# One of sixteen convolution taps per pass of the ConvFFN loop: from VectorE to ScalarE and GpSimd

## The chip, the cores and the metric

The kernel runs on one core of a Trainium2 chip. The metric is the device time of one execution in microseconds (us), as the median of several runs. The engines are TensorE (PE in the rows, its weight loads PEld), VectorE (DVE), ScalarE (ACT), GpSimd (POOL) and SyncE (SP), whose queue issues the DMAs spoken of here.

## What is computed

The kernel is one layer of a diffusion backbone: a token mixer (Fourier and gated recurrence), then a convolutional feed-forward block, then a final norm. The change lies in the feed-forward block:

```python
D_MODEL, SEQ, GRID_W, D_FF = 1024, 1024, 64, 2816     # 1024 tokens are a grid of 16 x 64

def dwconv2d(u, w, bias):          # 3x3, one filter per channel, zero padding
    ...
    return y + bias

def conv_ffn(h, rows, w_up, conv_w, conv_b, w_down):
    b, n, _ = h.shape
    u = (h @ w_up).reshape(b, rows, n // rows, 2 * D_FF)
    u = dwconv2d(u, conv_w, conv_b).reshape(b, n, 2 * D_FF)
    gate, val = jnp.split(u, 2, axis=-1)
    return (jax.nn.gelu(gate) * val) @ w_down
```

## The kernel before

The 2 x 2816 channels are handled in 22 pairs (`NP = 22`) of a gate tile and a value tile, each 128 channels by 1024 tokens. `ffn()` runs one **pass** n for each pair. A pass overlaps three stages of neighbouring pairs:

- **The product of pair n** (`up_product`, L1526). The up-projection of a gate and a value block is done by a Strassen-like scheme of seven products, i = 0 to 6, each of 12 matmuls (float32 split in a high and a low part). They go into two PSUM tiles, `ug` and `uv`, of which two pairs exist, so that pair n and pair n - 1 are held at once. Product 6 of a pair is made late, as the second product of the next pass. The order on TensorE in pass n is therefore (n,0), (n-1,6), (n,1), (n,2), (n,3), (n,4), (n,5). ScalarE copies some results (rows `ug<-ug`, `uv<-ug`, `p<-uv`, `u<-uv` of L131), and VectorE finishes each tile with one addition, the **join** (`up_join`, L1542): `ug<-ug,p` after product 4, `uv<-uv,u` after product 5. Product (n-1,6) waits for the join of `uv`.
- **The convolution of pairs n and n - 1** (`up_conv`, `conv`). ScalarE writes the centre tap and the bias into an accumulator in SBUF (L1552, for `uv` after product (n-1,6), for `ug` after the join). The other eight taps are `scalar_tensor_tensor` instructions on VectorE (L1564), which read PSUM and add into the accumulator. In pass n, VectorE runs: eight taps of the gate tile n - 1, five of the value tile n - 1, join of `ug`, three of the value tile n - 1, join of `uv`. Pass n is counted here from the join of `uv` of pair n - 1 to that of pair n.
- **The product of gate and value of pair n - 2** (`glu`, L1574): one GpSimd multiplication and a store of 512 KB to DRAM, `G<-s`, issued by SyncE.

Beside these, every pass prepares the weights of pair n + 1 (`up_split`): for each of the seven products ScalarE rounds 512 columns to float32r (`s<-s` of L131) and GpSimd subtracts to get the low part (L138). It also forms sums of weights of pair n + 2 on GpSimd (L1474, L1476, L1478, L1492) and loads two weight blocks (L1465).

**The slots.** Every tile in SBUF that these stages use (weights, their high and low parts, accumulators) takes one of 48 equal slots of 4 KB per partition (33 and 15, `Slots`). A freed slot goes to the end of a queue, and `get` takes the slot that has been free for longest. The order is fixed when the program is written, not at run time: an instruction that first writes a slot waits until all readers of its former tile are done, a store by DMA among them. In `glu` the value accumulator (`va`) and then the gate accumulator (`ga`) are given back; the last reader of `ga` is the store.

The order on each engine is the order in which this code issues its instructions; no scheduler moves them.

Of the kernel before, what the change touches and what calls it, by code (L numbers as in the profile page):

```python
# [10 lines left out]
AF = mybir.ActivationFunctionType  # L11
OP = mybir.AluOpType

S, D, C = 1024, 1024, 256
# [3 lines left out]
NP = FF // 128  # L18
# [94 lines left out]
class K:  # L113
# [1429 lines left out]

    def up_conv(self, n, x):
        u = self.U[n]
        u[x + "a"], u[x + "t"] = self.conv(u[x], n if x == "g" else NP + n)

    def conv(self, ps, ti):

        nc = self.nc  # L1550
        acc = self.sl.get([128, S], any_=True)
        nc.scalar.activation(acc, ps, AF.Identity, bias=self.par["fcb"][:, ti:ti + 1], scale=self.fcw(4, ti))  # L1552
        a3 = acc.rearrange("p (y x) -> p y x", y=GH)
        p3 = ps.rearrange("p (y x) -> p y x", y=GH)
        taps = deque()
        for dy in (-1, 0, 1):
            for dx in (-1, 0, 1):
                if dy == 0 and dx == 0:
                    continue
                y0, y1, x0, x1 = max(0, -dy), GH - max(0, dy), max(0, -dx), GW - max(0, dx)  # L1560
                o = a3[:, y0:y1, x0:x1]
                i = p3[:, y0 + dy:y1 + dy, x0 + dx:x1 + dx]
                taps.append(lambda o=o, i=i, w=self.fcw((dy + 1) * 3 + dx + 1, ti):
                            nc.vector.scalar_tensor_tensor(o, i, w, o, op0=OP.mult, op1=OP.add))  # L1564
        return acc, taps

    def gelu(self, n):
        g = self.U[n]["ga"]
# [2 lines left out]
    def glu(self, n):  # L1571

        nc, u = self.nc, self.U[n]
        nc.gpsimd.tensor_tensor(u["ga"], u["ga"], u["va"], op=OP.mult)  # L1574
        self.sl.free(u["va"])
        nc.sync.dma_start(self.G[n], u["ga"])
        self.sl.free(u["ga"])
        del self.U[n]
# [416 lines left out]
```

## Time and profile before

| | us |
|---|---|
| median of 3 runs | 1557.04 (1555.39 to 1558.95) |
| the profiled execution | 1557.34 |
| its span | 1555.5 |
| VectorE busy | 1215.6 (78%) |
| TensorE busy | 1408.2 (91%), granted clock 0.966 of full speed on average |
| GpSimd busy | 755.1 (49%) |
| ScalarE busy | 669.3 (43%) |

The feed-forward loop with its 22 pairs lies between about 835 us and 1275 us of the span. The shares over the whole span mix it with stages of other kinds, so the loop has to be read by itself, one pass at a time.

### The profile page before, as it was taken

To read this page: it belongs to the slowest core of one execution; us is meant where nothing else is said; L and a number is where in the kernel's file an instruction comes from. 1 tells how busy PE (TensorE), PEld (TensorE's weight loads), DVE (VectorE), ACT (ScalarE), POOL (GpSimd) and SP (SyncE) were. 2 spreads that over 40 slices of the span, in tenths; PEclk is the share of its full clock that TensorE was granted. 3 is DMA by queue.
4 is the path that set the end of the run, shared out by engine and by line. 5 is a ranking of instruction groups with operands and counts; after the bars stand their busy time and mean duration, and the time that the engine had idled before them with its cause. 6 is when DMAs were issued, how large, how long until landed. Compare 5 with 4: busy or idle time off the path is not lost.

```text
span 1555.5 us, 17031 instructions
## 1 busy us (share of the span) xinstructions
PE 1408.2 (91%) x6333; PEld 1126.9 (72%) x6333; DVE 1215.6 (78%) x1265; ACT 669.3 (43%) x968; POOL 755.1 (49%) x504
## 2 busy tenths in 40 slices
PE   5999999998999689979967999999999988989983
PEld 4788888877887678868845777777777767768862
DVE  5768677855116986495687999999999989799795
ACT  6566777663110213342255444444444434445441
POOL 2211311122002452392088777788777726886760
PEclk9999999999999899989988999999999998999996
DMA  9211111101115444413321112222211166422622
GB/s 374 94 34 34 35 34 41 41 28 55 41 54 180 136 126 160 154 41 122 111 80 54 66 61 78 82 82 82 82 63 64 51 243 230 183 75 102 230 88 103
DMA packets 52787, 155.21 MB, mean 100 GB/s; under 512 B 5781, under 2 KB 10192, under 8 KB 52704
## 3 DMA queue, kind: packets, MB, share of 16 engines
q1 hardware_dynamic: 51264, 151.76, 27.4%
q10 hardware_dynamic: 1184, 2.11, 0.4%
q8 instruction: 50, 0.82, 0.2%
q0 software_dynamic: 256, 0.25, 0.1%
q14 instruction: 33, 0.27, 0.1%
HBM read 131.29 MB, written 22.81 MB: 99 GB/s over the span
## 4 chain that ended last, share of the span: by engine, by line
DVE 36%; PE 13%; issue 6%; ACT 2%; POOL 1%; DMA 1%; SPq 0%; DVEq 0%; ACTq 0%; POOLq 0%
DVE s L1564 23%; PE big L194 6%; PE dn L1792 6%; DVE s L138 2%; POOL s L138 1%; DVE ug L1542 1%; DVE s L1713 1%; DVE uv L1542 1%; DVE s L1710 1%; DVE s L1225 1%; PE uv L1526 1%; DVE s L1784 1%; DMA s<-G 1%; ACT s L131 1%; DVE s L1726 1%
## 5 line engine op out<-in xcount | busy, mean ns | idle before, releaser
L138 POOL TENSOR_TENSOR s<-s,s 128x512 fp32r<-128x512 f32 (+1 forms) x288 | 462.0, 1621 | 332.4 <-ACT s L131 259.9
L194 PE MATMUL big<-s,s 128*128 128x512 f32 (+2 forms) x2352 | 559.2, 396 | 10.3 <-DVE s L138 6.5
L194 PEld LDWEIGHTS big<-s,s 128*128 128x128 f32 (+2 forms) x2352 | 438.0, 189 | 115.7 <-DVE s L138 7.8
L131 ACT ACTIVATE s<-s 128x512 fp32r<-128x512 f32 (+2 forms) x406 | 263.0, 697 | 259.8 <-DVE mid L912 61.9
L1526 PE MATMUL ug<-s,s 128*128 128x512 f32 x1056 | 263.9, 398 | 24.3 <-ACT uv L131 13.4
L138 DVE TENSOR_TENSOR s<-s,s 128x512 fp32r<-128x512 f32 (+2 forms) x150 | 189.8, 1274 | 92.1 <-ACT s L131 64.7
L1526 PEld LDWEIGHTS ug<-s,s 128*128 128x128 f32 x1056 | 197.7, 189 | 79.1 <-ACT uv L131 22.0
L1792 PE MATMUL dn<-s,s 128*128 128x512 f32 x924 | 227.9, 408 | 29.9 <-DVE s L138 15.5
L1792 PEld LDWEIGHTS dn<-s,s 128*128 128x128 f32 x924 | 180.0, 196 | 77.7 <-DVE s L138 17.5
L1564 DVE SCALAR_TENSOR_TENSOR s<-ug,rest,s 128x945 f32<-128x945 f32 (+2 forms) x176 | 214.9, 1221 | 5.3
L1564 DVE SCALAR_TENSOR_TENSOR s<-uv,rest,s 128x945 f32<-128x945 f32 (+2 forms) x176 | 214.8, 1220 | 4.6
L1526 PE MATMUL uv<-s,s 128*128 128x512 f32 x792 | 199.9, 402 | 15.3 <-DVE uv L1542 14.0
L1526 PEld LDWEIGHTS uv<-s,s 128*128 128x128 f32 x792 | 149.5, 191 | 59.1 <-DVE uv L1542 23.4
L782 POOL TENSOR_TENSOR s<-s,s 128x1280 f32<-128x1280 f32 x8 | 25.2, 3152 | 190.9 <-ACT s L778 190.9
L899 POOL TENSOR_TENSOR s<-s,s 128x1024 f32<-128x1024 f32 x8 | 21.1, 2641 | 127.4 <-PE big L194 120.7
L1474 POOL TENSOR_TENSOR s<-s,s 128x512 f32<-128x512 f32 x22 | 28.6, 1301 | 63.6 <-DMA s<-in_ffn_w_up_b_dram 63.6
L131 ACT ACTIVATE p<-uv 128x512 f32<-128x512 f32 x22 | 13.2, 599 | 105.5 <-PE uv L1526 105.5
L885 DVE TENSOR_TENSOR s<-big,s 128x1024 f32<-128x1024 f32 x8 | 9.8, 1224 | 61.1 <-PE big L194 61.1
L745 DVE SCALAR_TENSOR_TENSOR s<-big,par,s 128x1023 f32<-128x1023 f32 (+1 forms) x24 | 30.8, 1282 | 34.2 <-ACT s L742 33.6
L1574 POOL TENSOR_TENSOR s<-s,s 128x1024 f32<-128x1024 f32 x22 | 53.4, 2427 | 5.5 <-DVE s L1564 5.5
L1552 ACT ACTIVATE s<-uv,rest 128x1024 f32<-128x1024 f32 x22 | 26.6, 1208 | 48.2 <-POOL s L138 33.6
L777 ACT ACTIVATE s<-big,rest 128x1024 f32<-128x1024 f32 x32 | 35.7, 1117 | 24.6 <-PE big L194 17.8
(231 smaller groups left out, 1537.8 us busy)
## 6 DMA issues: line engine op xcount, KB each, us to landing
s<-in_mod_w_dram SPq DMA_DIRECT2D x48, 512.0 KB, 4.7
s<-in_ffn_w_up_b_dram SPq DMA_DIRECT2D x44, 512.0 KB, 4.3
s<-in_w_in_b_dram SPq DMA_DIRECT2D x32, 512.0 KB, 4.3
s<-G SPq DMA_DIRECT2D x55, 256.0 KB, 3.2
G<-s SPq DMA_DIRECT2D x22, 512.0 KB, 2.6
s<-in_ffn_w_down_dram SPq DMA_DIRECT2D x22, 512.0 KB, 5.8
s<-in_x_dram SPq DMA_DIRECT2D x16, 512.0 KB, 5.4
s<-G SPq DMA_DIRECT2D x11, 512.0 KB, 5.7
```

What stands on the lines that cost most here:

```text
L131: self.nc.scalar.activation(out, in_, AF.Copy)
L138: (self.nc.vector if eng == "dve" else self.nc.gpsimd).tensor_tensor(out, a, b, op=OP.subtract)
L194: return [lambda x=x: nc.tensor.matmul(x[0], x[1], x[2], start=x[3], stop=x[4]) for x in calls]
L745: nc.vector.scalar_tensor_tensor(u[:, lo:hi], z[:, lo + s:hi + s], tap[t], u[:, lo:hi], op0=OP.mult, op1=OP.add)
L777: nc.scalar.activation(lat, ps, AF.Sigmoid, bias=col)
L1474: p.tensor_tensor(u["x"][:, L], rg[:, L], rv[:, L], op=OP.subtract)
L1526: nc.tensor.matmul(o, x, y, start=first, stop=k == 3 and m == 2, skip_group_check=not fresh)
L1542: self.nc.vector.tensor_tensor(o, o, p, op=OP.add)
L1552: nc.scalar.activation(acc, ps, AF.Identity, bias=self.par["fcb"][:, ti:ti + 1], scale=self.fcw(4, ti))
L1564: nc.vector.scalar_tensor_tensor(o, i, w, o, op0=OP.mult, op1=OP.add))
L1574: nc.gpsimd.tensor_tensor(u["ga"], u["ga"], u["va"], op=OP.mult)
L1792: nc.tensor.matmul(bank[j], x, z, start=first and m == 0, stop=end and m == 2, skip_group_check=not check)
```

## The change

For the value tiles of pairs 0 to 20, the first of the eight taps (dy = -1, dx = -1: 15 rows of 63 elements, 945 per partition) is no longer a VectorE instruction. ScalarE multiplies the shifted PSUM tile by the tap's weight and writes the result into a slot of its own (`t`, L1567 of the new numbering, right behind the centre tap). GpSimd adds `t` to the accumulator at the beginning of `glu` (L1583), then multiplies as before (L1585), and `t` is given back ahead of `va` and `ga`. Pair 21 keeps all taps on VectorE.

```diff
     def up_conv(self, n, x):
         u = self.U[n]
-        u[x + "a"], u[x + "t"] = self.conv(u[x], n if x == "g" else NP + n)
-
-    def conv(self, ps, ti):
+        u[x + "a"], u[x + "t"], u[x + "r"] = self.conv(u[x], n if x == "g" else NP + n, x == "v" and n < NP - 1)
+
+    def conv(self, ps, ti, shared=False):
...
-        taps = deque()
+        taps, rest = deque(), None
...
+                if shared and rest is None:
+                    t = self.sl.get([128, S], any_=True)
+                    m = t[:, 0:(y1 - y0) * (x1 - x0)].rearrange("p (y x) -> p y x", y=y1 - y0)
+                    nc.scalar.activation(m, i, AF.Copy, scale=self.fcw((dy + 1) * 3 + dx + 1, ti))
+                    rest = o, m, t
+                    continue
...
-        return acc, taps
+        return acc, taps, rest
...
     def glu(self, n):
 
         nc, u = self.nc, self.U[n]
+        if u["vr"] is not None:
+            o, m, t = u["vr"]
+            nc.gpsimd.tensor_tensor(o, o, m, op=OP.add)
+            self.sl.free(t)
         nc.gpsimd.tensor_tensor(u["ga"], u["ga"], u["va"], op=OP.mult)
         self.sl.free(u["va"])
         nc.sync.dma_start(self.G[n], u["ga"])
```

The slots that the tiles get are other ones too, and with them the waits. On ScalarE, in the middle of the loop, one pass from the copy that follows product (n,1) stands as below before the change. `s1176`, `s1178`, `s1182`, `s1186` are the high parts of the weights for products 1 to 4 of the next pair; L1569 is the gelu, L1552 the centre tap of the gate tile, `u3` the copy that the join of `uv` needs. Names of semaphores in brackets say which engine or DMA queue an instruction waits for.

```order
L1552 ACTIVATE s1174_6810<-uv_6619,rest_93 128x1024 [waits DVE_49,PE_49,Pool_49]
L131 ACTIVATE uv_6766<-ug_6765 128x512 [waits PE_49]
L131 ACTIVATE s1176_6825<-s1160_6716 128x512 [waits Pool_49]
L131 ACTIVATE s1178_6840<-s1144_6620 128x512
L131 ACTIVATE p5_6858<-uv_6766 128x512 [waits PE_49,Activation_49]
L131 ACTIVATE s1182_6860<-s1145_6622 128x512
L131 ACTIVATE s1186_6882<-s1144_6620 128x512 [waits Pool_49]
L1569 ACTIVATE s1164_6741<-s1164_6741 128x1024 [waits DVE_49]
L1552 ACTIVATE s1188_6888<-ug_6765,rest_93 128x1024 [waits DMAHW4_49,DVE_49]
L131 ACTIVATE u3_6905<-uv_6766 128x512 [waits PE_49]
```

Here the wait for a DMA (`DMAHW4`, the store of `ga` of this pass's `glu`) stands at the centre tap `s1188`, whose slot was that `ga`. After the change the same place reads as follows; L1553 is the centre tap, L1567 the new tap, L1576 the gelu, and `s1188`, `s1190`, `s1195`, `s1199` are the high parts for products 1 to 4.

```order
L1553 ACTIVATE s1185_6821<-uv_6628,rest_93 128x1024 [waits DVE_49,PE_49]
L1567 ACTIVATE s1186_6823<-uv_6628,rest_93 128x945
L131 ACTIVATE uv_6777<-ug_6776 128x512 [waits PE_49]
L131 ACTIVATE s1188_6838<-s1171_6728 128x512 [waits Pool_49]
L131 ACTIVATE s1190_6853<-s1153_6629 128x512 [waits PE_49]
L131 ACTIVATE p5_6872<-uv_6777 128x512 [waits PE_49,Activation_49]
L131 ACTIVATE s1195_6874<-s1154_6631 128x512 [waits Pool_49]
L131 ACTIVATE s1199_6896<-s1153_6629 128x512 [waits DMAHW4_49,Pool_49]
L1576 ACTIVATE s1175_6753<-s1175_6753 128x1024 [waits DVE_49]
L1553 ACTIVATE s1201_6902<-ug_6776,rest_93 128x1024 [waits DVE_49]
L131 ACTIVATE u3_6918<-uv_6777 128x512 [waits PE_49]
```

Three waits are new: `s1190` waits for TensorE (its slot held the weights that product (n,2) of this very pass reads), `s1195` for GpSimd (its slot was `t`), and `s1199` for the store of `ga` of this pass's `glu`, whose slot it takes. The wait for the store has moved from the centre tap to an instruction ahead of the gelu.

On GpSimd, from the low part for product 2 on, the same stretch of a pass stands like this before the change (`L1574` is the multiplication of `glu`):

```order
L138 TENSOR_TENSOR s1178_6840<-s1144_6620,s1178_6840 128x512 [waits PE_49,Activation_49]
L1492 TENSOR_TENSOR s1144_6620<-s1144_6620,s1160_6716 128x512 [waits Pool_49]
L1574 TENSOR_TENSOR s1140_6594<-s1140_6594,s1150_6663 128x1024 [waits DMAHW6_49,DVE_49]
L138 TENSOR_TENSOR s1182_6860<-s1145_6622,s1182_6860 128x512 [waits PE_49,Activation_49]
L1474 TENSOR_TENSOR s1184_6863<-s1168_6767,s1169_6769 128x512 [waits DMAHW3_49,DMAHW2_49,PE_49]
L138 TENSOR_TENSOR s1186_6882<-s1144_6620,s1186_6882 128x512 [waits Activation_49]
```

and like this after it, with the new addition (L1583) ahead of the multiplication (L1585):

```order
L138 TENSOR_TENSOR s1216_7002<-s1179_6778,s1216_7002 128x512 [waits Activation_49]
L1492 TENSOR_TENSOR s1179_6778<-s1179_6778,s1197_6877 128x512 [waits Pool_49]
L1583 TENSOR_TENSOR s1185_6821<-s1185_6821,s1186_6823 128x15x63 [waits DVE_49]
L1585 TENSOR_TENSOR s1175_6753<-s1175_6753,s1185_6821 128x1024 [waits Pool_49]
L138 TENSOR_TENSOR s1221_7023<-s1180_6780,s1221_7023 128x512 [waits Activation_49]
L1474 TENSOR_TENSOR s1223_7026<-s1205_6927,s1206_6929 128x512 [waits DMAHW6_49,DMAHW5_49,Pool_49]
```

The multiplication, and the store behind it, stand one instruction later on GpSimd.

## Rows read from the trace of the kernel before

**Rows 1.** The page's chain that ended last, its shares by line.
```profile
DVE s L1564 23%; PE big L194 6%; PE dn L1792 6%; DVE s L138 2%; POOL s L138 1%; DVE ug L1542 1%; DVE s L1713 1%; DVE uv L1542 1%; DVE s L1710 1%; DVE s L1225 1%; PE uv L1526 1%; DVE s L1784 1%; DMA s<-G 1%; ACT s L131 1%; DVE s L1726 1%
```
**Rows 2.** Busy time by stretch, pass 7: engines with (instructions), PEclk, DMA, GB/s.
```profile
959.90:980.84 20.94, 20.01 (x86) 15.67 (x85) 20.48 (x20) 9.32 (x14) 16.50 (x13) 1.00 0.21 76
```
**Rows 3.** Timeline, VectorE, joins of `uv` of pairs 0, 6, 21: start, duration.
```profile
834.26 0.70 DVE L1542 TENSOR_TENSOR uv<-uv,u 128x512 f32<-128x512 f32 x1 [2.80 <-ACT u L131]
...
959.90 0.69 DVE L1542 TENSOR_TENSOR uv<-uv,u 128x512 f32<-128x512 f32 x1
...
1273.95 0.69 DVE L1542 TENSOR_TENSOR uv<-uv,u 128x512 f32<-128x512 f32 x1
```
**Rows 4.** Timeline, VectorE, pass 7: start, duration, merged instructions (xcount).
```profile
960.49 10.02 DVE L1564 SCALAR_TENSOR_TENSOR s<-ug,rest,s 128x945 f32<-128x945 f32 x8
...
970.42 6.29 DVE L1564 SCALAR_TENSOR_TENSOR s<-uv,rest,s 128x945 f32<-128x945 f32 x5
...
976.63 0.69 DVE L1542 TENSOR_TENSOR ug<-ug,p 128x512 f32<-128x512 f32 x1
...
977.23 3.68 DVE L1564 SCALAR_TENSOR_TENSOR s<-uv,rest,s 128x945 f32<-128x945 f32 x3
```
**Rows 5.** Timeline, TensorE, pass 7; in brackets the idle time before and its releaser.
```profile
960.64 3.06 PE L1526 MATMUL uv<-s,s 128*128 128x512 f32 x12 [0.26 <-DVE uv L1542]
...
967.12 3.04 PE L1526 MATMUL ug<-s,s 128*128 128x512 f32 x12 [0.67 <-ACT uv L131]
...
978.29 2.96 PE L1526 MATMUL ug<-s,s 128*128 128x512 f32 x12
```
**Rows 6.** Timeline, ScalarE, pass 7.
```profile
963.78 1.21 ACT L1552 ACTIVATE s<-uv,rest 128x1024 f32<-128x1024 f32 x1 [1.72 <-POOL s L138]
966.48 0.58 ACT L131 ACTIVATE uv<-ug 128x512 f32<-128x512 f32 x1 [1.49 <-PE ug L1526]
...
966.98 1.14 ACT L131 ACTIVATE s<-s 128x512 fp32r<-128x512 f32 x2
...
973.01 0.60 ACT L131 ACTIVATE p<-uv 128x512 f32<-128x512 f32 x1 [4.90 <-PE uv L1526]
973.51 1.15 ACT L131 ACTIVATE s<-s 128x512 fp32r<-128x512 f32 x2
...
974.55 1.05 ACT L1569 ACTIVATE s<-s 128x1024 f32<-128x1024 f32 x1
...
977.36 1.21 ACT L1552 ACTIVATE s<-ug,rest 128x1024 f32<-128x1024 f32 x1 [1.76 <-DVE ug L1542]
...
978.49 0.60 ACT L131 ACTIVATE u<-uv 128x512 f32<-128x512 f32 x1
```
**Rows 7.** Timeline, GpSimd, pass 7, up to the multiplication of `glu`.
```profile
967.67 2.56 POOL L138 TENSOR_TENSOR s<-s,s 128x512 fp32r<-128x512 f32 x2 [3.50 <-ACT s L131]
...
970.32 1.30 POOL L1492 TENSOR_TENSOR s<-s,s 128x512 f32<-128x512 f32 x1
...
971.57 2.41 POOL L1574 TENSOR_TENSOR s<-s,s 128x1024 f32<-128x1024 f32 x1
```
**Rows 8.** Timeline, SyncE, the store of pass 7.
```profile
974.00 0.33 SPq L1576 DMA_DIRECT2D G<-s  x1
```
**Rows 9.** Landing of the `G` stores issued from 940 to 1000 us.
```profile
DMA to landing us min/median/max: 2.7/2.7/2.7
```
**Rows 10.** Landing of all 44 loads of up-projection weights.
```profile
DMA to landing us min/median/max: 3.3/4.3/5.9
```
**Rows 11.** Timeline, TensorE after pauses: behind joins of pairs 1 and 21; in down-projection.
```profile
855.95 3.01 PE L1526 MATMUL uv<-s,s 128*128 128x512 f32 x12 [3.05 <-DVE uv L1542]
...
1274.70 4.50 PE L1526 MATMUL uv<-s,s 128*128 128x512 f32 x12 [3.04 <-DVE uv L1542]
...
1335.21 5.09 PE L1792 MATMUL dn<-s,s 128*128 128x512 f32 x14 [3.80 <-POOL s L138]
```
**Rows 12.** Busy time by stretch after the last of these pauses; PEclk is 0.66.
```profile
1335.00:1340.00 5.00, 4.79 (x14) 3.77 (x15) 0.00 (x0) 1.31 (x3) 5.00 (x5) 0.66 0.69 236
```

## The prediction

> **What bounds the kernel now.** I read the chain that ended last first. Its largest share, 23% of the span, is VectorE in the taps of L1564 [rows 1], so the feed-forward loop is where VectorE sets the time. Then I read one pass by itself. The joins of `uv` come at 834.26 for pair 0 and 1273.95 for pair 21 [rows 3]: 21 passes of (1273.95 - 834.26) / 21 = 20.94 us. In pass 7 VectorE is busy for 20.48 of 20.94 us, TensorE for 20.01, GpSimd for 16.50 and ScalarE for 9.32, at full TensorE clock [rows 2]. VectorE has no gap to speak of: eight taps, five taps, join, three taps, and the next join follow each other [rows 4]. TensorE is close behind, with two short waits in a pass, 0.26 us for the join of `uv` and 0.67 us for ScalarE's copy [rows 5]. So there is a little under a microsecond a pass to be had before TensorE takes over, and GpSimd and ScalarE look as if they had room. Whether they have it at the right place is the question, and the answer lies in the slots.
>
> **What is taken from VectorE.** One of sixteen taps in a pass. Eight taps take 10.02 us, three 3.68 [rows 4], so a tap is worth 1.25 us, and 21 pairs give 26 us at the very most. TensorE allows less: without its wait for the join a pass still lasts about 20.94 - 0.6 = 20.3 us (the wait is 0.26 us, and the first matmuls restart some 0.3 us late behind it [rows 5]; 0.3 is my estimate). That is 0.6 us a pass, 13 us in all, if nothing else gets in the way.
>
> **What ScalarE gets.** One activation of 945 elements from PSUM. The nearest row is the centre tap, 1024 elements in 1.21 us [rows 6]; by elements 1.1 us. It stands behind the centre tap, which starts at 963.78, and ends near 963.78 + 1.21 + 1.1 = 966.1, while the next copy can start only at 966.48, when product (n,1) is done; ScalarE idles there now for 1.49 us [rows 6]. Cost: nothing, with 0.4 us to spare. If the strided read took over 1.5 us, the rest would be paid in every pass.
>
> **What GpSimd gets.** One addition of 945 elements. The multiplication of `glu` has the same two inputs and 1024 elements: 2.41 us [rows 7], so by elements 2.2 us; 2.4 if the size counts for nothing, and a strided output could make it dearer. GpSimd has 20.94 - 16.50 = 4.4 us free in a pass [rows 2], so its total fits. But the multiplication, and the store of `ga` behind it, come later by this.
>
> **What happens to the slots.** This is the part that decides. `t` is held from the second product of a pass to the `glu` of the next one, longer than a pass, so between those places two more slots are out. The order of ScalarE's instructions shows what follows: the high part for product 2 now waits for product (n,2) itself, and the high part for product 4 waits for the store of `ga` of the same pass. Before, that store was waited for by the centre tap of the gate tile, which starts at 977.36 behind the join of `ug` [rows 6]; the store, issued at 974.00 [rows 8], had landed after 2.7 us [rows 9], at 976.7. So it was hidden, by 0.7 us. ScalarE takes its instructions in order: the copies at 973.51 run right behind `p<-uv`, for which it idled 4.90 us [rows 6]. Whatever is queued behind a waiting copy waits too. Behind the high part for product 4 stand gelu, the centre tap of the gate tile and `u<-uv`, and for the last the join of `uv` waits, on which product (n,6) of TensorE waits.
>
> **The new chain, one pass, in the times of pass 7.**
> - From the join at 959.90 [rows 3], products (6,6) and (7,1), and then (7,2), which starts at 967.12 and takes 3.04 us [rows 5]: done at 970.2.
> - Copy for product 2, 0.57 (half of two that take 1.14 [rows 6]): 970.8. Before it ran at 967.55.
> - GpSimd: the low part 1.28 (half of 2.56), L1492 1.30 [rows 7], and some 0.1 until GpSimd sees the copy: 973.4. The new addition 2.2: 975.6. The multiplication 2.41: 978.0. Before, the multiplication ended at 974.0.
> - Store, 2.7 us to landing [rows 9]: 980.8.
> - ScalarE: copy for product 4, 0.6; gelu 1.05; centre tap 1.21; `u<-uv` 0.60 [rows 6]: 984.2.
> - VectorE: join of `uv`, near 984.3. It has idled by then for some 4 us, its two taps long done.
>
> So a pass takes 984.3 - 959.9 = 24.4 us, and 24.4 - 20.94 = 3.5 us more than before. The chain closes on itself (join, products, copy, GpSimd, store, ScalarE, join), so it is paid each time. The bounds of the chain: 3.0 us if the addition and the hand-overs take half a microsecond less; 4.1 us if the store lands after 3.3 us, the least of the weight loads [rows 10], since a load is now issued right behind the store and both move at once.
>
> **How often.** The store is waited for where two weight blocks are still being loaded, in passes 2 to 19, 18 times. 18 x 3.5 = 63 us. Passes 1, 20 and 21 have the relief of VectorE without the wait, some 1 us each; the last `glu` delays the first of the down-projection by part of 2.2 us. Together I take -2 us.
>
> **TensorE's clock.** In the new pass TensorE ends product (8,0), which starts at 978.29 and takes 2.96 [rows 5], at 981.25 as now, and then stands until the join at 984.3 is done: until 985.05, a pause of 3.8 us. The trace has pauses of this size. Behind one of 3.80 us the granted clock is 0.66 of full speed over the 5 us that follow [rows 11, 12], that is 2 x 0.34 x 5 = 3.4 us at 1.2 in place of 2.4 GHz, which costs 1.7 us of work. Behind one of 3.04 us a product of 12 matmuls takes 4.50 us, behind one of 3.05 us another takes 3.01 [rows 11]: near 3 us it falls or it doesn't. The products behind the pause are those at the head of the chain, so what they lose lengthens the pass. Bounds: nothing, and 2.4 us if two such stretches follow each other. I take 1.5 us, close to the 1.7 of the row that has the same pause and a little less, since part of the slow stretch can fall into the pause itself: 18 x 1.5 = 27 us.
>
> The Trainium skill ("TensorE: Matmul & The Clock Gate", section "HAM oscillation — how this bites in real kernels") describes a loop whose every step leaves TensorE waiting and which therefore loses its clock anew in every step. By that rule the fall comes in all 18 passes, as I have it; without it the sum would be 27 us less. The three pauses above agree for about 3.8 us, and leave it open for 3 us.
>
> **The sum.** 1557.3 (the profiled execution, 0.3 above the median) + 63 + 27 - 2 = 1645 us.
>
> **The rivals.**
> - *The chain holds, the clock doesn't fall* (or seldom): 1557.3 + 63 - 2 = 1618. For it speaks the full-speed product behind the pause of 3.05 us; against it the pause of 3.80 us. If the chain is shorter by 0.7 us, its pause is near 3 us and this is what comes.
> - *The waits are hidden and VectorE's relief shows*: faster. It would need the store to have landed by about 977.4, when the centre tap of the gate tile starts now, 3.4 us ahead of my 980.8: GpSimd would have to do addition and multiplication with hardly any time above what the multiplication takes now. Then TensorE at 20.3 us a pass bounds, 1557.3 - 21 x 0.6 = 1544, or at best the whole tap, 1531. For it speaks that VectorE is the bound in the trace and that GpSimd and ScalarE are idle for a fifth and a half of a pass; against it, that every step of the chain has a row.
> - *The exchange is even*: the chain is only as long as the old pass, 20.9 us, and the time stays within 0.2%. It takes the same shortfall of over 3 us less a bit, so it is less likely still.
>
> **How the numbers follow.** Forecast 0.63, at 1645; clock stays up 0.25, at 1618; relief shows 0.10; even 0.02. A measurement of this kernel can tell about 0.2% from no change. Faster 0.10, within it 0.02, slower 0.88. The range reaches over both slow cases: from 18 x 3.0 - 4 = 50 above the execution, 1607, to the longer chain with the dearer clock, 18 x (4.1 + 2.4) = 117 above, 1674; I cut that to 1670, since both ends together are unlikely.
>
> **What would show it.** In the profile after: joins of `uv` some 26 us apart in place of 20.94; VectorE idle before this join, released by ScalarE's `u<-uv`; ScalarE idle for over 4 us before one `s<-s` copy in each pass, released by the store of `G`; TensorE pausing near 4 us before `uv`, released by that join; a granted clock below 1 within the loop in most passes. If passes are 24.4 us apart at full clock, the second case holds. If joins are 20.3 us apart or less and ScalarE does not wait for the store, the prediction is wrong, and the wrong step is the duration on GpSimd or the landing of the store. If the new activation runs past 966.5 in pass 7's times, its cost was not nothing.

## The result and the profile after

The changed kernel takes 1656.17 us in the median of 4 runs (1654.83 to 1658.93), the kernel before 1556.93 in the same comparison. The ratio is 1.064, with a 95% interval from 1.0626 to 1.0654: slower by 99 us. The prediction was 1645 us, slower, from 1607 to 1670.

The profiled execution has a span of 1653.2 us, 97.7 us more than before. The page's busy times (us, share of the span, number of instructions) show that no engine has become the bound by its own work. VectorE is busy for 19 us less than before (the 21 taps that it no longer makes took 25), and now stands idle more:

```profile
PE 1447.7 (88%) x6333; PEld 1154.8 (70%) x6333; DVE 1196.4 (72%) x1244; ACT 691.9 (42%) x989; POOL 795.1 (48%) x525
```

The shares of the chain that ended last have changed more than the busy times. The taps, 23% of the span before [rows 1], are down to 1% (L1571), and the store of the product tile, the additions and the multiplication on GpSimd and TensorE's products have come in:

```profile
PE ug L1526 8%; PE uv L1526 7%; PE dn L1803 6%; PE big L194 5%; DMA G<-s 3%; POOL s L138 3%; POOL s L1585 3%; POOL s L1583 2%; DVE s L138 2%; ACT s L131 2%; POOL s L1492 1%; ACT s L1553 1%; DVE s L1571 1%; ACT s L1576 1%; DVE uv L1542 1%
```

The joins of `uv` on VectorE (start, duration, in brackets the idle time before and its releaser) give the length of the passes:

```profile
852.38 0.69 DVE L1542 TENSOR_TENSOR uv<-uv,u 128x512 f32<-128x512 f32 x1
876.77 0.70 DVE L1542 TENSOR_TENSOR uv<-uv,u 128x512 f32<-128x512 f32 x1 [4.61 <-ACT u L131]
903.87 0.70 DVE L1542 TENSOR_TENSOR uv<-uv,u 128x512 f32<-128x512 f32 x1 [5.32 <-ACT u L131]
...
1330.20 0.70 DVE L1542 TENSOR_TENSOR uv<-uv,u 128x512 f32<-128x512 f32 x1 [5.08 <-ACT u L131]
1350.96 0.70 DVE L1542 TENSOR_TENSOR uv<-uv,u 128x512 f32<-128x512 f32 x1 [0.30 <-ACT u L131]
1371.35 0.70 DVE L1542 TENSOR_TENSOR uv<-uv,u 128x512 f32<-128x512 f32 x1 [0.30 <-ACT u L131]
```

From pair 1 to pair 19 there are 18 passes, (1330.20 - 852.38) / 18 = 26.55 us each, where it was 20.94 [rows 3]. In each of them VectorE idles for 4.6 to 5.8 us before this join, waiting for ScalarE's copy `u<-uv`. The last two passes, which have no weights to load any more, take 20.76 and 20.39 us. So the whole loss is in 18 passes: 18 x (26.55 - 20.94) = 101 us.

Where the copy was held up is seen in pass 8, on ScalarE, GpSimd, SyncE and VectorE (the row of the tap first, then the end of the pass):

```profile
1017.17 1.04 ACT L1567 ACTIVATE s<-uv,rest 128x945 f32<-128x945 f32 x1
...
1022.91 0.63 ACT L131 ACTIVATE s<-s 128x512 fp32r<-128x512 f32 x1 [2.60 <-PE ug L1526]
1023.62 1.29 POOL L138 TENSOR_TENSOR s<-s,s 128x512 fp32r<-128x512 f32 x1 [1.95 <-ACT s L131]
1024.99 1.30 POOL L1492 TENSOR_TENSOR s<-s,s 128x512 f32<-128x512 f32 x1
...
1026.25 2.02 POOL L1583 TENSOR_TENSOR s<-s,s 128x945 f32<-128x945 f32 x1
...
1028.35 2.41 POOL L1585 TENSOR_TENSOR s<-s,s 128x1024 f32<-128x1024 f32 x1
...
1030.79 0.33 SPq L1587 DMA_DIRECT2D G<-s  x1
...
1033.76 0.63 ACT L131 ACTIVATE s<-s 128x512 fp32r<-128x512 f32 x1 [4.82 <-DMA G<-s]
1034.29 1.04 ACT L1576 ACTIVATE s<-s 128x1024 f32<-128x1024 f32 x1
...
1035.24 1.18 ACT L1553 ACTIVATE s<-ug,rest 128x1024 f32<-128x1024 f32 x1
...
1036.33 0.58 ACT L131 ACTIVATE u<-uv 128x512 f32<-128x512 f32 x1
...
1036.94 0.70 DVE L1542 TENSOR_TENSOR uv<-uv,u 128x512 f32<-128x512 f32 x1 [5.35 <-ACT u L131]
```

Read it as one chain: ScalarE's copy for product 2 waits for TensorE, GpSimd does four instructions behind it, SyncE stores, ScalarE waits 4.82 us for that store with its copy for product 4, and only then come gelu, centre tap, the last copy and the join. The waits of the whole loop (us in total, times, longest) say that the wait for the store comes 18 times, once in each of these passes:

```profile
DVE uv L1542 <- ACT u L131: 99.2, 21, 5.8
ACT s L131 <- DMA G<-s: 86.8, 18, 5.3
```

TensorE pauses behind the join in each pass, and its first products after the pause are slow (pass 8, then pass 9):

```profile
1010.54 5.49 PE L1526 MATMUL uv<-s,s 128*128 128x512 f32 x12 [3.70 <-DVE uv L1542]
...
1015.82 3.34 PE L1526 MATMUL ug<-s,s 128*128 128x512 f32 x12
...
1037.70 4.33 PE L1526 MATMUL uv<-s,s 128*128 128x512 f32 x12 [3.72 <-DVE uv L1542]
```

The busy times by stretch (the engines as in [rows 2], then granted clock, DMA share, GB/s) show a full clock in pass 2, whose head follows no such pause, and put it at 0.89 over passes 3 to 19, from 876.77 on. It differs from pass to pass (pass 8, then pass 9):

```profile
852.38:876.77 24.39, 19.97 (x84) 15.62 (x84) 19.36 (x19) 9.95 (x15) 18.39 (x13) 1.00 0.14 46
876.77:1330.20 453.43, 378.88 (x1428) 294.19 (x1428) 330.82 (x290) 177.78 (x256) 311.40 (x222) 0.89 0.18 58
1009.78:1036.94 27.16, 22.77 (x84) 17.66 (x84) 19.46 (x17) 10.46 (x16) 18.30 (x14) 0.87 0.17 59
1036.94:1062.61 25.67, 21.28 (x84) 16.59 (x84) 19.46 (x18) 10.46 (x16) 18.32 (x14) 0.93 0.19 62
```

### The profile page after: what moved, and what is told of

Same layout as the page of the kernel before. It is cut to its first block, busy times and chain, and to the rows that moved or that the text cites. A ratio compares the mean times of both kernels' runs of the same rounds, so it can differ in the third digit from the quotient of the medians.

```text
span 1653.2 us, 17018 instructions
## 1 busy us (share of the span) xinstructions
PE 1447.7 (88%) x6333; PEld 1154.8 (70%) x6333; DVE 1196.4 (72%) x1244; ACT 691.9 (42%) x989; POOL 795.1 (48%) x525
## 4 chain that ended last, share of the span: by engine, by line
PE 28%; DVE 11%; POOL 10%; ACT 6%; DMA 4%; issue 4%; SPq 0%; ACTq 0%; POOLq 0%; DVEq 0%
PE ug L1526 8%; PE uv L1526 7%; PE dn L1803 6%; PE big L194 5%; DMA G<-s 3%; POOL s L138 3%; POOL s L1585 3%; POOL s L1583 2%; DVE s L138 2%; ACT s L131 2%; POOL s L1492 1%; ACT s L1553 1%; DVE s L1571 1%; ACT s L1576 1%; DVE uv L1542 1%
## 5 line engine op out<-in xcount | busy, mean ns | idle before, releaser
L131 ACT ACTIVATE s<-s 128x512 fp32r<-128x512 f32 (+2 forms) x406 | 268.9, 698 | 438.5 <-DMA G<-s 86.8
L1526 PE MATMUL uv<-s,s 128*128 128x512 f32 x792 | 235.3, 454 | 73.0 <-DVE uv L1542 71.7
L1526 PE MATMUL ug<-s,s 128*128 128x512 f32 x1056 | 268.8, 403 | 24.4 <-ACT uv L131 13.4
L1526 PEld LDWEIGHTS ug<-s,s 128*128 128x128 f32 x1056 | 202.7, 194 | 82.6 <-ACT uv L131 22.2
L1526 PEld LDWEIGHTS uv<-s,s 128*128 128x128 f32 x792 | 173.1, 222 | 124.5 <-DVE uv L1542 80.7
L1571 DVE SCALAR_TENSOR_TENSOR s<-ug,rest,s 128x945 f32<-128x945 f32 (+2 forms) x176 | 214.9, 1221 | 5.3
L1571 DVE SCALAR_TENSOR_TENSOR s<-uv,rest,s 128x945 f32<-128x945 f32 (+2 forms) x155 | 189.4, 1222 | 3.9
L1542 DVE TENSOR_TENSOR uv<-uv,u 128x512 f32<-128x512 f32 x22 | 15.4, 699 | 99.2 <-ACT u L131 99.2
L899 POOL TENSOR_TENSOR s<-s,s 128x1024 f32<-128x1024 f32 x8 | 21.2, 2654 | 128.5 <-PE big L194 120.5
L1585 POOL TENSOR_TENSOR s<-s,s 128x1024 f32<-128x1024 f32 x22 | 53.7, 2442 | 7.1 <-DVE s L1571 5.5
L1553 ACT ACTIVATE s<-uv,rest 128x1024 f32<-128x1024 f32 x22 | 26.6, 1207 | 71.9 <-PE uv L1526 71.9
```

Source lines behind the costliest of these rows:

```text
L131: self.nc.scalar.activation(out, in_, AF.Copy)
L1526: nc.tensor.matmul(o, x, y, start=first, stop=k == 3 and m == 2, skip_group_check=not fresh)
L1542: self.nc.vector.tensor_tensor(o, o, p, op=OP.add)
```

## The experiments

Theory: two slots fewer between the value tile's tap and the multiplication move two waits into ScalarE's queue; with the multiplication one addition later they close a chain that is longer than the old pass, and TensorE's pause in it costs clock. Rivals: the later multiplication alone; the work on ScalarE and GpSimd; a chain that is long for another reason, with the clock beside it. Seven kernels tell them apart. The passes below are means over passes 2 to 19, from the joins of pairs 1 and 19, unless another stretch is named.

**1. The clock taken out.** The changed kernel with TensorE kept at work in its pause:

```diff
+                    if i == 6 and 1 < n < last:
+                        for _ in range(13):
+                            self.up_touch(n, "v1")
                     self.up_product(m, i)
```

> The changed kernel with 13 matmuls more in passes 2 to 20, between product (n,0) and product (n-1,6), where TensorE pauses; they write half a PSUM tile that product (n,3) overwrites, so the result is the same. They last some 3.0 of the 3.7 us pause. Theory (chain of waits plus the clock that falls in the pause): the clock stays at 2.4 GHz, the pass is the chain alone, 24.0 to 24.4 us in place of 26.55: 1656 - 18 x 2.3 = 1615 us. Rival (the slow clock lies beside the chain and costs nothing, the chain itself is 26.5 us long): 1656, or some us more for the matmuls.

Measured: 1619.17 us, ratio to the kernel before 1.0392 (1.0377 to 1.0408). The 13 matmuls fill the pause, the product behind them takes its usual time (TensorE), and the clock over the loop is full (busy times by stretch):

```profile
1022.52 3.11 PE L1513 MATMUL uv<-s 128*128 128x512 f32 x13
1026.40 3.04 PE L1526 MATMUL uv<-s,s 128*128 128x512 f32 x12 [0.77 <-DVE uv L1542]
```

```profile
880.00:1310.00 430.00, 405.45 (x1712) 318.80 (x1713) 344.43 (x303) 185.73 (x267) 326.43 (x231) 1.00 0.19 61
```

The joins of pairs 2 and 19, 17 passes apart. Pass 2 itself took 26.79 us here and is left out: there is no such pause yet at its head, so its 13 matmuls lengthen it.

```profile
879.32 0.70 DVE L1542 TENSOR_TENSOR uv<-uv,u 128x512 f32<-128x512 f32 x1 [5.37 <-ACT u L131]
...
1293.74 0.70 DVE L1542 TENSOR_TENSOR uv<-uv,u 128x512 f32<-128x512 f32 x1 [4.32 <-ACT u L131]
```

(1293.74 - 879.32) / 17 = 24.38 us a pass. That is the chain without the clock, and it agrees with the 24.39 us of the changed kernel's own pass 2, at full clock. The clock's part of the changed kernel's pass is 26.55 - 24.38 = 2.17 us, 18 x 2.17 = 39 us, and the two medians differ by 37. More work on TensorE makes this kernel faster. The rival of a clock that lies beside the chain is out.

**2. The slot alone.** The kernel before, all taps on VectorE, with a slot held as `t` is:

```diff
+        if x == "v" and n < NP - 1:
+            u["vr"] = self.sl.get([128, S], any_=True)
+            self.nc.scalar.activation(u["vr"][:, 0:1], u["va"][:, 0:1], AF.Copy)
...
+        if "vr" in u:
+            self.sl.free(u["vr"])
         nc.gpsimd.tensor_tensor(u["ga"], u["ga"], u["va"], op=OP.mult)
```

> The kernel before with nothing moved: all eight taps stay on VectorE. Only the slot is held as t is in the changed kernel, from the value tile's centre tap to the multiplication two stages later; ScalarE writes one element per partition into it. Theory (two slots fewer between these places put the waits for product (n,2) and for the store into ScalarE's queue): the chain of the changed kernel without its addition. The changed kernel's pass without its slow clock is near 24.05 us (a pass of 25.67 us, less 1.6 by which its first product is slow), less 2.04 us for the addition: a pass of 22.0 us in place of 20.94, 18 times, 1557 + 19 = 1576 us; TensorE's pause is then near 1.5 us and the clock stays up. Rival 1 (the later multiplication is the cause, the slots are harmless): 1557. Rival 2 (the work given to ScalarE and GpSimd is the cause): 1557.

Measured: 1589.79 us, ratio 1.0215 (1.0184 to 1.0246): slower, as the theory has it and neither rival does, but by 32 us in place of 19. Joins of pairs 1 and 19 on VectorE, and the store and the copy that waits for it in one pass:

```profile
854.52 0.69 DVE L1542 TENSOR_TENSOR uv<-uv,u 128x512 f32<-128x512 f32 x1
...
1260.34 0.70 DVE L1542 TENSOR_TENSOR uv<-uv,u 128x512 f32<-128x512 f32 x1 [0.88 <-ACT u L131]
```

```profile
985.93 0.33 SPq L1581 DMA_DIRECT2D G<-s  x1
...
988.88 0.63 ACT L131 ACTIVATE s<-s 128x512 fp32r<-128x512 f32 x1 [4.76 <-DMA G<-s]
```

The pass is 22.55 us on average. Twelve of the 18 last 22.0 to 22.4, near the 22.0 that I had: the copy starts 2.95 us after the issue of the store, where the chain counted 2.7 [rows 9]. In five the store lands later, the copy starts 3.45 to 4.08 us after its issue, and the pass takes 22.8 to 23.4 us; the longest one, 23.79 us, has a granted clock of 0.93. What the late stores have in common is told in the last section. A slot that nobody reads, held for a pass and a bit, costs this kernel 2%.

**3. The later multiplication alone.** The kernel before, no slot held, one operation more on GpSimd:

```diff
+        if n < NP - 1:
+            o = u["va"].rearrange("p (y x) -> p y x", y=GH)[:, 1:, 1:]
+            nc.gpsimd.tensor_tensor(o, o, o, op=OP.add)
         nc.gpsimd.tensor_tensor(u["ga"], u["ga"], u["va"], op=OP.mult)
```

> The kernel before with nothing moved and no slot held, and an addition of 945 elements ahead of the multiplication on GpSimd; it adds the value accumulator to itself, so 945 elements of each value tile are doubled in the result. Theory (the later multiplication hurts only through the slots): the store lands near 978.8 in the times of pass 7, the centre tap of the gate tile waits for it and ends 1.5 us later, and the join of uv is ready at 980.8, just where VectorE gets to it anyway: 1557 us, at most 1560. Rival 1 (the addition on GpSimd costs its 2.04 us in each pass by itself): 1557 + 18 x 2.04 = 1594.

Measured: 1564.09 us, ratio 1.0040 (1.0025 to 1.0055). Almost hidden, as forecast, though not quite: 6 us and not 3 at the most. The operation, whose two inputs are the same tile, takes 1.76 us; the changed kernel's addition takes 2.02. In most passes the centre tap of the gate tile waits for the store a little over a microsecond (first row) and the pass keeps its 20.94 us; in a few the store is late, the longest case here (rows two and three: issued at 955.74, waited for until 961.00), and those passes take up to 23.0 us; the pass behind the longest takes 22.0 at a granted clock of 0.92:

```profile
983.01 1.21 ACT L1552 ACTIVATE s<-ug,rest 128x1024 f32<-128x1024 f32 x1 [1.20 <-DMA G<-s]
```

```profile
955.74 0.33 SPq L1579 DMA_DIRECT2D G<-s  x1
...
961.00 1.20 ACT L1552 ACTIVATE s<-ug,rest 128x1024 f32<-128x1024 f32 x1 [3.67 <-DMA G<-s]
```

The rival that the addition costs its 2 us in each pass by itself is out.

**4. Both, with nothing taken from VectorE.** The slot of 2 and the operation of 3 together:

```diff
+            o = u["va"].rearrange("p (y x) -> p y x", y=GH)[:, 1:, 1:]
+            nc.gpsimd.tensor_tensor(o, o, o, op=OP.add)
             self.sl.free(u["vr"])
```

> The kernel before with all taps on VectorE, with the slot held as t is and the extra operation on GpSimd ahead of the multiplication (945 elements of each value tile are doubled in the result). Nothing is taken from VectorE and no tap is made by ScalarE. Theory (only the two together make the long chain, and VectorE's relief buys nothing in it): the chain is that of the changed kernel, 24.4 us less 0.3 since this operation took 1.76 us and not 2.04, and TensorE pauses by 3.4 us, so the clock falls in most passes: some 26 us a pass, 1645 us. Rival (the two prices just add): 1557 + 32 + 6 = 1595.

Measured: 1646.32 us, ratio 1.0570 (1.0552 to 1.0588). The two prices, 32 and 6 us, do not add to 38 but make 89. Joins of pairs 1 and 19, and the busy times by stretch with a clock of 0.92:

```profile
853.38 0.69 DVE L1542 TENSOR_TENSOR uv<-uv,u 128x512 f32<-128x512 f32 x1
...
1315.78 0.70 DVE L1542 TENSOR_TENSOR uv<-uv,u 128x512 f32<-128x512 f32 x1 [3.56 <-ACT u L131]
```

```profile
880.00:1330.00 450.00, 378.58 (x1469) 294.67 (x1468) 362.66 (x316) 166.28 (x260) 314.73 (x228) 0.92 0.17 58
```

A pass is 25.69 us. Pass 2, still at full clock, takes 24.01, for which the theory had 24.1. In 2 the operation is not in the chain, in 3 it ends beside VectorE's work; only where ScalarE's copy waits for the store does each microsecond on GpSimd lengthen the pass, and with it TensorE's pause until the clock falls. This kernel has VectorE's whole work and is still within 10 us of the changed one: in such a pass the relief of VectorE buys nothing.

**5. The addition early, the slot given back at once.** The changed kernel with the addition right behind ScalarE's tap:

```diff
-                    rest = o, m, t
+                    nc.gpsimd.tensor_tensor(o, o, m, op=OP.add)
+                    self.sl.free(t)
+                    rest = ()
                     continue
```

> The changed kernel with the addition on GpSimd moved: it stands right behind ScalarE's tap, before VectorE's taps of that tile, and t is given back there at once. Tap and addition are all done as in the changed kernel. Theory (the slot held over a pass is the cause, the exchange of work itself is good): the store is waited for by the gate tile's centre tap again, the high part for product 2 no longer waits for product (n,2); TensorE bounds a pass at 20.3 to 20.4 us, 18 x 0.55 + some 2 us for passes 1, 20 and 21: 1545 us. Rival 1 (the later multiplication is the cause): also some 1545, since the multiplication is only 0.6 us late. Rival 2 (ScalarE's and GpSimd's added work is the cause): above 1557, since all of it is still done.

Measured: 1542.31 us, ratio 0.9900 (0.9883 to 0.9916). The same tap by ScalarE, the same addition by GpSimd, and the kernel is faster than the one before by 1%. Joins of pairs 1 and 21 on VectorE, then the addition and the centre tap that waits for the store again, but only for 1.23 us:

```profile
853.66 0.69 DVE L1542 TENSOR_TENSOR uv<-uv,u 128x512 f32<-128x512 f32 x1
...
1261.37 0.70 DVE L1542 TENSOR_TENSOR uv<-uv,u 128x512 f32<-128x512 f32 x1 [0.28 <-ACT u L131]
```

```profile
983.58 2.02 POOL L1568 TENSOR_TENSOR s<-s,s 128x945 f32<-128x945 f32 x1 [1.36 <-ACT s L1567]
...
994.72 1.21 ACT L1553 ACTIVATE s<-ug,rest 128x1024 f32<-128x1024 f32 x1 [1.23 <-DMA G<-s]
```

(1261.37 - 853.66) / 20 = 20.39 us a pass, the pace of TensorE that the prediction put at 20.3: from 976.34 to 996.70 it is busy for 19.69 us, and the rest is its wait of 0.67 us for ScalarE's copy. The rival that the exchanged work is the cause is out.

**6. The addition early, the slot held.** One difference to 5:

```diff
                     nc.gpsimd.tensor_tensor(o, o, m, op=OP.add)
-                    self.sl.free(t)
-                    rest = ()
+                    rest = t
...
+        if u["vr"] is not None:
+            self.sl.free(u["vr"])
```

> The kernel that adds early, with one difference: t is given back at the multiplication, two stages later, and not right behind the addition. Theory (the held slot is the cause, wherever the addition stands): the waits for product (n,2) and for the store are back in ScalarE's queue, the multiplication is not delayed, so the passes are those of the run that only holds a slot, near 22.4 us: 1585 us. Rival (it was the early place of the addition that brought 1542, by the earlier multiplication): 1542 to 1546.

Measured: 1587.06 us, ratio 1.0186 (1.0166 to 1.0206). The joins of pairs 1 and 19:

```profile
853.60 0.69 DVE L1542 TENSOR_TENSOR uv<-uv,u 128x512 f32<-128x512 f32 x1
...
1267.72 0.70 DVE L1542 TENSOR_TENSOR uv<-uv,u 128x512 f32<-128x512 f32 x1 [2.19 <-ACT u L131]
```

A pass is 23.0 us on average. Ten of the 18 last 22.0 to 22.3, as in 2; in the others the store lands late, or the granted clock is 0.87 to 0.93, and they take up to 25.0. Between this kernel and 5 no instruction is added or taken away; the 45 us between them are the time at which a slot is given back. So it was not the early place of the addition that won 1%.

**7. Another owner for the slot that the store frees.** The changed kernel, `ga`'s slot given back behind the gate tile's centre tap:

```diff
-        self.sl.free(u["ga"])
+        self.stored.append(u["ga"])
...
                     self.up_conv(n, "g")
+                    while self.stored:
+                        self.sl.free(self.stored.pop())
```

> The changed kernel, with one difference: the slot of ga is given back behind the centre tap of the gate tile and not right behind the store is issued, so the store is waited for by a later weight load and not by ScalarE's copy for product 4. The other new waits stay. Theory (the wait for the store is the link that closes the chain): ScalarE's gelu, centre tap and last copy no longer stand behind the store. The centre tap's slot is now freed by GpSimd's low part behind the multiplication, near 979.2 in the times of pass 7, so the join of uv comes near 981.1: a pass of 21.2 us, a pause of TensorE under 1 us, the clock up, 1557 + 18 x 0.3 - 2 = 1560 us. Rival (the wait for product (n,2) or for the addition is what costs): 1640 or more.

Measured: 1561.21 us, ratio 1.0027 (1.0017 to 1.0036): of the 99 us that the change cost, 95 are gone, with the wait for product (n,2), the wait for the addition and the late multiplication all in place. ScalarE's centre tap now waits for GpSimd's low part behind the multiplication, and no longer for the store (pass 7); joins of pairs 1 and 19 below:

```profile
1000.36 1.21 ACT L1553 ACTIVATE s<-ug,rest 128x1024 f32<-128x1024 f32 x1 [1.67 <-POOL s L138]
```

```profile
853.46 0.69 DVE L1542 TENSOR_TENSOR uv<-uv,u 128x512 f32<-128x512 f32 x1
...
1235.56 0.70 DVE L1542 TENSOR_TENSOR uv<-uv,u 128x512 f32<-128x512 f32 x1 [1.44 <-ACT u L131]
```

A pass is 21.23 us; 21.2 was forecast by the same way of adding rows. The wait for the store is the link that closes the long chain.

## Why the prediction was right, point by point

- **What bounds before.** VectorE with TensorE close behind: right. Where ScalarE's copies no longer wait for the store (run 5), a pass is 20.39 us, for which 20.3 was worked out.
- **What ScalarE gets.** Forecast 1.1 us and hidden; the tap takes 1.04 us, and run 5 makes it in every pass and is faster.
- **What GpSimd gets.** Forecast 2.2 us; 2.02 in pass 8. By itself it is nearly hidden, 6 us in run 3.
- **The slots.** Right, and shown from both sides: held without any use they cost 32 us (run 2), and given back early or handed to another they cost nothing or little (runs 5 and 7).
- **The chain.** Forecast 24.4 us a pass, 24.38 in run 1, 18 x (24.38 - 20.94) = 62 us against 63 in the sum. Part of this agreement is luck, since two steps were off and made up for each other. From the start of the copy for product 2 to the store it is 7.88 us in pass 8 (1022.91 to 1030.79), as in the forecast (7.8: the addition is 0.2 us shorter, the hand-overs are that much longer). The copy for product 4 then starts 2.97 us after the store's issue (1030.79 to 1033.76), not 2.7, and from there to the join it is 3.18 us (to 1036.94), not 3.5. The bound of 3.3 from the weight loads [rows 10] was the right direction for the store; a load is issued 0.4 us behind it now.
- **How often.** 18 waits for the store, as forecast. The passes without it: pass 1 19.70, pass 20 20.76, pass 21 20.39, together 62.8 - 60.85 = 2.0 us less than three old passes, against the -2 in the sum. The late last `glu`, which I had counted in, costs next to nothing: from the join of pair 21 to the end of the span it is 281.9 us, and was 281.6.
- **The clock.** This term was mis-sized: 1.5 us a pass, 27 in all; it is 2.17 and 39, and that is the 11 us by which the forecast fell short. I sized it from one pause of 3.80 us with 3.4 us at the lower clock behind it [rows 11, 12]. Over passes 3 to 19, from 876.77 on, 0.89 of full speed is 2 x 0.11 x 453.43 = 100 us at 1.2 GHz, some 5.9 us for each of 17 passes (between 5.6 and 6.1 by the rounding of 0.89). In pass 9 it is 2 x 0.07 x 25.67 = 3.6 us, as I had it; in pass 8 2 x 0.13 x 27.16 = 7.1, twice that, and the product takes 5.49 and not 4.33 us. Against 24.38 us, six of the 17 passes lose 1.3 to 1.6 us (passes of 25.67 to 25.94 us), the size that I forecast, and eleven lose 2.6 us or more (26.93 to 27.62). That is above the 2.4 us that stood in the prediction as the bound for two slow stretches; two of the 1.7 us of the row would have been 3.4. The pauses ahead of passes 8 and 9 are 3.70 and 3.72 us, so their length does not tell the two sizes apart; what does stays open. By the rule of the Trainium skill that was weighed there ("TensorE: Matmul & The Clock Gate", section "HAM oscillation — how this bites in real kernels") the fall comes again in every step; the trace agrees, with a granted clock of 0.87 to 0.93 in each of passes 3 to 20.
- **The rivals.** "The clock doesn't fall" would have been 1618; run 1 makes that case, 1619, of which 2.4 us are its pass 2 (26.79 in place of 24.39). "Relief shows" was to need the store 3.4 us ahead of 980.8, which is 20.9 us after the join. In run 5 it is waited for until 18.4 us after the join (976.34 to 994.72), 2.5 us ahead, and by the centre tap alone; that is enough, and the time is 1542, for which 1544 was worked out.

The sum, mended: 1557.3 + 62 + 39 - 2 = 1656. So the forecast was right by its mechanism: the chain's term came out within 1 us, and the clock's had the right cause and two thirds of its size.

## What to carry to other kernels

Before work is moved to an idle engine, look at what it passes its result in: a buffer from a pool that is nearly used up changes who gets which buffer, and so who waits for whom, in parts of the kernel that the change doesn't touch. An in-order engine must not get a buffer whose last reader is a store that this engine's own later results have to come before; give the buffer back as soon as the result is added in, or hand it to a load. Where a chain closes on itself over a pass, time added anywhere in it is paid in every pass, and if it makes TensorE pause by some microseconds, as by 3.7 here, the clock is to be counted too, with its own range.

## What was not expected of the hardware

- A pause of TensorE of 3.7 us in each pass costs more than one such pause in isolation showed: from 3.6 to 7.1 us at the lower clock, where 3.4 had been read [rows 12]. Filling it with 13 matmuls that nobody reads made the kernel 37 us faster (run 1). A shorter pause can do it too, and need not: ahead of pass 2 TensorE pauses by 1.77 us in run 6, and the granted clock from 856 to 858 us is 0.50; it pauses by 1.78 us at the same place in the changed kernel, and the clock of pass 2 is 1.00.
- The store of 512 KB lands a little later when a load is issued right behind it. Where the load follows by 0.4 us, the copy that waits starts 2.95 and 2.97 us after the store's issue (run 2 and the changed kernel); where it follows by 1.3 us, the waiting centre tap starts 2.82 us after it (run 5).
- GpSimd's addition with a strided output of 15 x 63 elements is not dearer by the element than the dense multiplication: 2.02 us for 945 elements, 2.41 for 1024.
- Now and then a store lands far later, in run 3 5.26 us after its issue (955.74 to 961.00). The DMA view shows one thing that these cases share, a transfer on a queue of the kind `instruction` (below for 955.74 to 961.00: number, MB, share). In the changed kernel and runs 1 to 6, 122 stores issued between 850 and 1280 us are waited for, and 16 of the waits end over 3.3 us after the issue. All 16 have such a transfer between 0.3 us ahead of the issue and the end of the wait; of the other 106, five have one. That it delays the store is likely by this, and not shown: no run takes it away.

```profile
q8 instruction: 1, 0.02, 2.4%
```
